# A two-layer hybrid encoder step on one core: the gate and up quadrants are loaded through GpSimd's queue

## The chip, the cores and the metric

The kernel runs on 1 of the 8 cores of one Trainium2 chip. The metric is the device time of one execution in microseconds (us). Engines are named as the profile names them: PE is TensorE's matmul side and PEld its weight load, DVE is VectorE, ACT is ScalarE, POOL is GpSimd, SP is SyncE. SP and POOL also have queues from which loads from HBM are issued.

## The reference

A step of a streaming encoder for 560 frames (512 new ones, 32 of a running stream, 16 meta frames) with a model width of 1024. Two layers, a GLA mixer and an MLA mixer, each stand between two half-step SwiGLU blocks; all is float32. The SwiGLU block is what the change touches:

```python
def swiglu_half(h, norm_w, w_gate, w_up, w_down):
    hn = rmsnorm(h, norm_w)
    return h + 0.5 * ((jax.nn.silu(hn @ w_gate) * (hn @ w_up)) @ w_down)
# per layer i: swiglu_half (ffn1), mixer (GLA for i = 0, MLA for i = 1), swiglu_half (ffn2); D_FF = 2816
```

## The kernel before, in words

Frames lie on the free dimension, features on the 128 partitions; the residual `h` stays on the core. A float32 product is made of three passes on float32r halves: every weight tile is cut into `whi` (ACT, line 331) and `wlo` (DVE, line 332, the rest after `whi`), both from pools of four buffers, and `mm` (line 370) multiplies whi by x-high (line 378), wlo by x-high (379) and whi by x-low (381).

**The four FFNs.** `ffn(1,0)`, `ffn(2,0)`, `ffn(1,1)` and `ffn(2,1)` run in this order, with the GLA mixer between the first two and the MLA mixer between the last two. Each has 11 steps of `gate_up` (line 467), two 128-column tiles of the hidden layer at a time. A step is a Strassen-like product: seven products of quadrants instead of eight. `quads` (line 435) brings the four quadrants r11, r12, r21, r22 of gate and up weights (each a tile `fr` of 128 x 1024 float32, 512 KB, loaded by `quadrant`, line 354, as two DMAs of 128 x 512, one for gate and one for up), adds them on DVE (line 451, four adds `fr<-fr` per step) and yields seven weight tiles in turn. The tiles `fr` come from a pool of six buffers, and each step takes five (the fifth holds a sum), so the load of a quadrant waits until DVE has finished with an earlier tile in that buffer.

**Down weights.** `down` (line 544) is cut into 16 pieces per group of steps; each loads its weights through `load` (line 334) into a tile `raw` (two buffers) and adds into `h` (line 556). The pieces of a group are woven between the products of the next group (`between`, line 579). The groups have 2, 4, 4, 4 and 8 tiles of the hidden layer; the first is one step long, and the pieces of the first group are short. The first two quadrants of a later FFN are also loaded ahead into `raw` tiles by `first_weights` (line 348).

**Queues.** All weight loads, quadrants and `raw` alike, are issued by SP, one after the other. An instruction on a queue that waits for its buffer holds up all that stand behind it there. POOL issues no load; it has some 110 small instructions in the two mixers (lines 616 to 645, 753 to 788, 913, 955, 1033, 1067, 1118 to 1123). ACT issues some constants and outputs. The scheduler of the language sets the final order on each engine, so that SP's quadrant loads and `raw` loads alternate within a step.

Of the kernel before, what the change touches and what calls it, by code (L numbers as in the profile page):

```python
# [289 lines left out]
class Net:  # L290
# [61 lines left out]
        return self.whole(raw)  # L352

    def quadrant(self, t, i, l, f, q):
        for j, x in enumerate("gu"):
            off, n = PLAN[x, i, l, f + q // 2]
            src = self.a["W"][off:off + P * n].rearrange("(p k c) -> p k c", p=P, k=2)[:, q % 2]
            self.nc.sync.dma_start(t[:, 512 * j:512 * j + 512], src)

    def whole(self, src):  # L360
        hi = self.w.tile([P, 8, P], F32R, name="whi", tag="whi")
# [1208 lines left out]
```

## Time and profile before

| what | value |
|---|---|
| median of 3 runs | 2117.19 us (2110.93 to 2117.34) |
| time of the profiled execution | 2109.41 us |
| its span, first to last instruction | 2107.5 us |
| outside the span | 1.9 us |
| PE busy, share of the span | 2026.0 us, 96% |
| DVE busy | 1643.2 us, 78% |
| ACT busy | 1018.4 us, 48% |
| POOL busy | 51.4 us, 2% |
| granted TensorE clock, mean | 0.982 |
| loads of 128 x 512 quadrant halves | 352 `fr<-W` and 12 `raw<-W`, 256 KB each |

The profile is of one execution, and all times within it are microseconds from the start of its span. A group row has the source line, the engine, the operation, the tiles out<-in, the shape and the count, then the busy time and the mean of one in ns, then the engine's idle time before them and what ended it. "SPq" is SP's queue. A line of the chain of waits has the start, the length and what was running. A row of the waits has the total in us, how many times, and the longest. The mixers lie at about 380 to 690 us and 1420 to 1720 us; the FFNs are the rest.

### The profile page before, as it was taken

How to read it: one execution, taken by the hardware profiler on the slowest of the kernel's cores; microseconds unless marked ns; L12 is line 12 of the kernel's file. 1: busy time of each engine (PE TensorE's matmuls, PEld its weight loads, DVE VectorE, ACT ScalarE, POOL GpSimd, SP SyncE). 2: the span in 40 equal slices, each digit the busy share in tenths (PEclk: the TensorE clock that was granted, in tenths of full speed). 3: DMA queues.
4: the chain of work that ended last, by engine and by line, in shares of the span. 5: the costliest groups of instructions: out<-in, count | busy, mean ns of one | idle time of the engine just before them, and what ended most of it. 6: DMA issues, size and time to landing. Idle time of an engine off the chain costs nothing.

```text
span 2107.5 us, 38039 instructions
## 1 busy us (share of the span) xinstructions
PE 2026.0 (96%) x15290; PEld 1980.2 (94%) x15290; DVE 1643.2 (78%) x3097; ACT 1018.4 (48%) x1822; POOL 51.4 (2%) x117
## 2 busy tenths in 40 slices
PE   5999999999999899999989999999999979999997
PEld 5999999989999799999979999999988969999997
DVE  8887878556658888788778877886788788878884
ACT  6444445455445444445545444454575454444451
POOL 0000000101110000000000000000210000000000
PEclk8999999999999899999989999999999989999998
DMA  3323222222221332322222322222211223232221
GB/s 131 106 87 107 93 96 78 77 68 71 73 80 55 108 103 82 106 86 91 81 95 96 105 92 91 95 83 92 61 51 59 71 86 100 90 111 91 96 72 62
DMA packets 93633, 183.29 MB, mean 87 GB/s; under 512 B 10433, under 2 KB 22081, under 8 KB 93457
## 3 DMA queue, kind: packets, MB, share of 16 engines
q1 hardware_dynamic: 89632, 176.24, 26.1%
q10 hardware_dynamic: 3824, 4.63, 0.7%
q8 instruction: 120, 1.97, 0.4%
q14 instruction: 57, 0.46, 0.1%
HBM read 176.84 MB, written 3.99 MB: 86 GB/s over the span
## 4 chain that ended last, share of the span: by engine, by line
PE 82%; DVE 10%; ACT 3%; DMA 2%; issue 2%; SPq 0%; POOL 0%; DVEq 0%; ACTq 0%; POOLq 0%
PE Y L381 8%; PE Y L378 8%; PE Y L379 8%; PE A L379 5%; PE A L381 5%; PE A L378 5%; PE ps L378 4%; PE ps L381 4%; PE ps L379 4%; PE B L378 3%; PE B L379 3%; PE B L381 3%; PE C L379 3%; PE C L381 3%; PE C L378 3%; DVE wlo L332 3%
## 5 line engine op out<-in xcount | busy, mean ns | idle before, releaser
L332 DVE TENSOR_TENSOR wlo<-fr,whi 128x1024 fp32r<-128x1024 f32 x302 | 363.9, 1216 | 17.2 <-ACT whi L331 17.0
L378 PE MATMUL Y<-ah,whi 128*128 128x280 f32 (+1 forms) x1408 | 373.8, 291 | 1.9 <-ACT ah L331 1.0
L379 PE MATMUL Y<-ah,wlo 128*128 128x280 f32 (+1 forms) x1408 | 373.4, 292 | 0.0
L331 ACT CAST whi<-fr 128x1024 fp32r<-128x1024 f32 x302 | 313.3, 1049 | 92.9 <-PE C L381 34.6
L378 PE MATMUL A<-x,whi 128*128 128x280 f32 (+1 forms) x1056 | 286.3, 296 | 29.5 <-ACT whi L331 29.5
L379 PE MATMUL A<-x,wlo 128*128 128x280 f32 (+1 forms) x1056 | 285.7, 296 | 1.0 <-DVE wlo L332 1.0
L378 PEld LDWEIGHTS Y<-ah,whi 128*128 128x128 f32 x1408 | 265.2, 188 | 3.4 <-ACT ah L331 1.7
L556 DVE SCALAR_TENSOR_TENSOR h<-Y,h 128x280 f32<-128x280 f32 (+1 forms) x320 | 140.9, 443 | 161.9 <-PE Y L381 161.2
L379 PEld LDWEIGHTS Y<-ah,wlo 128*128 128x128 f32 x1408 | 265.4, 188 | 0.0
L332 DVE TENSOR_TENSOR wlo<-raw,whi 128x512 fp32r<-128x512 f32 (+5 forms) x237 | 203.6, 861 | 76.7 <-ACT whi L331 71.9
L331 ACT CAST whi<-raw 128x512 fp32r<-128x512 f32 (+5 forms) x237 | 176.0, 744 | 173.4 <-PE ps L381 55.2
L381 PE MATMUL Y<-al,whi 128*128 128x280 f32 (+1 forms) x1408 | 233.9, 292 | 0.0
L378 PEld LDWEIGHTS A<-x,whi 128*128 128x128 f32 x1056 | 203.9, 193 | 31.1 <-ACT whi L331 31.1
L451 DVE TENSOR_TENSOR fr<-fr 128x1024 f32<-128x1024 f32 x176 | 214.5, 1219 | 20.4 <-DMA fr<-W 18.1
L379 PEld LDWEIGHTS A<-x,wlo 128*128 128x128 f32 x1056 | 203.7, 193 | 1.7 <-DVE wlo L332 1.4
L381 PEld LDWEIGHTS Y<-al,whi 128*128 128x128 f32 x1408 | 201.2, 189 | 0.0
L378 PE MATMUL B<-x,whi 128*128 128x280 f32 (+1 forms) x704 | 188.6, 293 | 3.4 <-ACT whi L331 3.4
L379 PE MATMUL C<-x,wlo 128*128 128x280 f32 (+1 forms) x704 | 187.1, 292 | 3.5 <-DVE wlo L332 3.5
L379 PE MATMUL B<-x,wlo 128*128 128x280 f32 (+1 forms) x704 | 187.4, 292 | 0.8 <-DVE wlo L332 0.8
L378 PE MATMUL C<-x,whi 128*128 128x280 f32 (+1 forms) x704 | 187.4, 291 | 0.6 <-ACT whi L331 0.6
L381 PE MATMUL A<-x,whi 128*128 128x280 f32 (+1 forms) x1056 | 181.2, 294 | 0.0
L490 ACT COPY r<-A 128x560 f32<-128x560 f32 (+1 forms) x132 | 82.2, 623 | 174.1 <-PE A L381 173.8
(368 smaller groups left out, 4059.2 us busy)
## 6 DMA issues: line engine op xcount, KB each, us to landing
fr<-W SPq DMA_DIRECT2D x352, 256.0 KB, 3.4
raw<-W SPq DMA_DIRECT2D x80, 512.0 KB, 3.5
raw<-W SPq DMA_DIRECT2D x112, 256.0 KB, 2.9
raw<-W SPq DMA_DIRECT2D x40, 128.0 KB, 2.1
h<-xT SPq DMA_DIRECT2D x3, 560.0 KB, 7.6
raw<-W SPq DMA_DIRECT2D x4, 384.0 KB, 3.1
o_y<-h SPq DMA_DIRECT2D x8, 136.0 KB, 2.2
o_y<-h ACTq DMA_DIRECT2D x8, 136.0 KB, 1.9
```

Of the source, the lines that this page charges most:

```text
L331: self.nc.scalar.copy(hi, src)
L332: self.nc.vector.tensor_tensor(lo, src, hi.bitcast(F32), op=ALU.subtract)
L378: f(hi[:, b0 + k, :], xh[:, c], start=not more and k == 0, stop=False)
L379: f(lo[:, b0 + k, :], xh[:, c], start=False, stop=False)
L381: f(hi[:, b0 + k, :], xl[:, c], start=False, stop=k == n - 1)
L451: add = lambda out, x, y: nc.vector.tensor_tensor(out, x, y, op=ALU.add)
L490: nc.scalar.copy(r[:, :, :n], of[:, :, :n])
L556: nc.vector.scalar_tensor_tensor(self.h[:, m, c], Y[:, :n], 0.5, self.h[:, m, c], op0=ALU.mult, op1=ALU.add)
```

## The change

`quadrant` chooses a queue. Only the four quadrants of the very first step (`ffn(1,0)`, f = 0) stay on SP; all other quadrant halves, those of `first_weights` among them, are issued by POOL. Down weights, mixer weights and the inputs stay on SP. Sizes, tiles, buffers and arithmetic are as before. The lines below 355 move down by two, so 358 becomes 360.

```diff
     def quadrant(self, t, i, l, f, q):
+
+        queue = self.nc.sync if (i, l, f) == (1, 0, 0) else self.nc.gpsimd
         for j, x in enumerate("gu"):
             off, n = PLAN[x, i, l, f + q // 2]
             src = self.a["W"][off:off + P * n].rearrange("(p k c) -> p k c", p=P, k=2)[:, q % 2]
-            self.nc.sync.dma_start(t[:, 512 * j:512 * j + 512], src)
+            queue.dma_start(t[:, 512 * j:512 * j + 512], src)
```

SP's queue around the start of `ffn(2,0)`, before (W is the packed weight array; `fr` is a quadrant, `raw` a down or mixer weight, or a quadrant where line 358 stands):

```order
L341 DMA raw<-W 128x1024 x28
L358 DMA raw<-W 128x512 x4
L341 DMA raw<-W 128x1024 x2
L341 DMA raw<-W 128x256 x2
L358 DMA fr<-W 128x512 x18
L341 DMA raw<-W 128x256
L358 DMA fr<-W 128x512
L341 DMA raw<-W 128x256
L358 DMA fr<-W 128x512 x2
L341 DMA raw<-W 128x256
L358 DMA fr<-W 128x512 x2
L341 DMA raw<-W 128x256
```

The same queue at the same place now:

```order
L341 DMA raw<-W 128x816 x2
L341 DMA raw<-W 128x544
L341 DMA raw<-W 128x1024 x30
L341 DMA raw<-W 128x256 x8
L341 DMA raw<-W 128x512 x24
L341 DMA raw<-W 128x1024 x8
```

The quadrants are gone from it, and the `raw` loads stand one behind the other in the same order.

POOL's queue at the head of the program, before (the first rows of work are the constants of the GLA mixer, some 360 us into the run):

```order
L1561 MEMSET const-uint8-127 128x1
L1566 UNCONDITIONAL_BRANCH [waits barrier_Pool_Activation_PE_DVE_SP_gather]
L616 MEMSET aT_4687 128x128 [waits DVE_49,PE_49,Activation_49]
L616 MEMSET aT_4688 128x128
L616 MEMSET aT_4689 128x128
```

And now:

```order
L1563 MEMSET const-uint8-127 128x1
L1568 UNCONDITIONAL_BRANCH [waits barrier_Pool_Activation_PE_DVE_SP_gather]
L360 DMA fr<-W 128x512 x2
L360 DMA fr<-W 128x512 [waits DVE_49]
L360 DMA fr<-W 128x512
L360 DMA fr<-W 128x512 [waits DMAHW3_49,DMAHW4_49,DVE_49,Activation_49]
L360 DMA fr<-W 128x512
```

The first quadrant of the second step (f = 2) has no wait before it, and stands at the head of POOL's queue from the start of the run; on SP it stood behind the inputs and the whole first step.

POOL's queue at the turn from the MLA mixer to `ffn(2,1)`, before: the last copies of the mixer, and then nothing to the end.

```order
L1123 CAST qrs<-x 64x32 [waits DVE_49,Pool_49]
L1118 CAST ptl<-x 128x32 [waits DVE_49,Pool_49]
L1118 CAST pth<-x 128x32 [waits Activation_49]
L1118 CAST ptl<-x 128x32 [waits DVE_49]
L1566 UNCONDITIONAL_BRANCH
```

And now (the names behind "waits" are semaphores of engines and of earlier loads, DMASW those of POOL's own):

```order
L360 DMA raw<-W 128x512
L360 DMA fr<-W 128x512 [waits DMASW4_49,DVE_49,PE_49]
L360 DMA fr<-W 128x512 [waits DMASW5_49]
L360 DMA fr<-W 128x512 x2
L360 DMA fr<-W 128x512 [waits DMASW0_49]
L360 DMA fr<-W 128x512 [waits DMASW1_49]
L360 DMA fr<-W 128x512 [waits DMASW2_49]
L360 DMA fr<-W 128x512 [waits DMASW3_49]
L360 DMA fr<-W 128x512 [waits DMASW4_49,Pool_49]
L360 DMA fr<-W 128x512 [waits DMASW5_49]
L360 DMA fr<-W 128x512 [waits DMASW6_49,DVE_49]
```

The eight halves of the first step's four quadrants stand on POOL one after the other behind a single wait for room, as they stood on SP. The sequences of PE, DVE and ACT are the same as before but for a few neighbours that change places in some steps.

## Prediction

> **What bounds the kernel now.** First the page's head: which engine is full. Then the busy time in each FFN (the four windows are `ffn(1,0)`, `ffn(2,0)`, `ffn(1,1)`, `ffn(2,1)` without their ends; columns: length, busy time and count of PE, PEld, DVE, ACT, POOL, then clock, DMA share, GB/s).
>
> ```profile
> span 2107.5 us, 38039 instructions
> PE 2026.0 (96%) x15290; PEld 1980.2 (94%) x15290; DVE 1643.2 (78%) x3097; ACT 1018.4 (48%) x1822; POOL 51.4 (2%) x117
> 50.00:435.00 385.00, 381.28 (x2918) 377.82 (x2919) 299.77 (x463) 180.57 (x300) 9.45 (x27) 0.99 0.28 91
> 745.00:1080.00 335.00, 332.20 (x2569) 331.65 (x2567) 269.67 (x414) 156.33 (x241) 0.00 (x0) 1.00 0.29 93
> 1080.00:1420.00 340.00, 332.35 (x2545) 331.14 (x2546) 279.83 (x410) 159.68 (x248) 0.18 (x1) 0.98 0.29 93
> 1715.00:2080.00 365.00, 351.74 (x2774) 350.24 (x2774) 291.06 (x439) 167.08 (x261) 0.00 (x0) 0.98 0.30 95
> ```
>
> PE is busy for 97 to 99% of these stretches, at 0.98 to 1.00 of its clock, while loads keep the DMA engines busy for 0.28 to 0.30. DVE is the second: 80 to 82%. So the question is not how long SP's queue waits, but whether PE ever waits for a quadrant. Next the waits: PE's largest, SP's two largest, and DVE's for quadrants.
>
> ```profile
> PE A L378 <- ACT whi L331: 29.5, 6, 8.8
> SPq L341 <- DVE wlo L332: 826.0, 159, 30.4
> SPq L358 <- DVE wlo L332: 517.2, 109, 24.0
> DVE fr L451 <- DMA fr<-W: 18.1, 16, 2.5
> ```
>
> SP waits 1343 us at the two load lines, but for DVE to free a buffer, and another queue has to wait for the same buffers. DVE waits 18.1 us for quadrants in 16 places. PE's 29.5 us are six waits, and by their places they lie at the start of an FFN:
>
> ```profile
> PE A L378 <- ACT whi L331: 15.3, 2, 8.8
> PE A L378 <- ACT whi L331: 3.8, 1, 3.8
> PE A L378 <- ACT whi L331: 6.2, 1, 6.2
> ```
>
> 15.3 us lie in the first 25 us of the run, 3.8 us each at the start of `ffn(2,0)` and `ffn(1,1)`, 6.2 us at that of `ffn(2,1)`. In the middle of an FFN PE does not wait for loads. The change can hardly win time there; what it can lose is the margin of the few loads that come in just in time.
>
> **What a load costs on POOL.** The change moves 356 of 364 loads of 128 x 512 (352 `fr` and 12 `raw`, less the 8 of the first step) from SP to POOL. SP issues one in about 0.43 us:
>
> ```profile
> fr<-W SPq DMA_DIRECT2D x352, 256.0 KB, 3.4
> L358 SPq DMA_DIRECT2D fr<-W x10: 327/430/500, 1713.7 to 1717.8; - x10
> DMA to landing us min/median/max: 2.9/5.9/6.8
> ```
>
> The ten loads at the start of `ffn(2,1)` take 327 to 500 ns each to issue; the quickest is down 2.9 us after the start of its issue, so 2.6 us after its end. The trace has no load on POOL. The nearest rows are POOL's own instructions on 128 x 512:
>
> ```profile
> 443.44 1.04 POOL L788 TENSOR_TENSOR qS<-qg,fac 128x512 f32<-128x512 f32 x1
> 448.27 1.24 POOL L788 TENSOR_TENSOR kS<-kd,fac 128x512 f32<-128x512 f32 x1 [3.79 <-DVE kd L781]
> ```
>
> I bound one issue on POOL by 0.43 us below (no dearer than on SP) and 1.24 us above, and take 1.04 us, the nearer of POOL's own rows, what it takes over a tile of this size undisturbed; SP's row is another engine's. In an FFN 88 loads come in 335 us or more, one in 3.8 us, so POOL is no bottleneck by rate.
>
> [...]
>
> **Part by part.** (1) *Start of the run.* POOL's first two loads wait for nothing, so 512 KB for the second step enter the DMA engines beside the inputs and the first quadrants.
>
> ```profile
> 2.66 5.00 DMA fr<-W
> 7.74 1.04 ACT whi L331
> 3.00:15.00 12.00, 5.51 (x27) 5.20 (x28) 7.50 (x14) 9.58 (x19) 0.00 (x0) 1.00 1.02 339
> ```
>
> The chain starts with a quadrant half that lands at 7.66 us and its cast at 7.74; from 3 to 15 us the DMA engines are full (share 1.02, 339 GB/s). 524,288 bytes at 339 GB/s are 1.55 us, which the first quadrant and the inputs come later if POOL's loads share the engines with them. Between 0 and 1.55 us; I take +1.5, since the chain is DMA and its users up to PE's start.
>
> (2) *The tight place of each FFN.* In the third and fourth step the short down pieces fill little PE time and DVE has no rest. There one quadrant's buffer comes free late. The chain in `ffn(1,1)`, then DVE and PE as they go on:
>
> ```profile
> 1149.31 1.24 DVE wlo L332
> 1150.57 0.33 SPq L358
> 1150.94 3.88 DMA fr<-W
> 1154.89 1.24 DVE fr L451
> 1158.96 1.22 DVE L332 TENSOR_TENSOR wlo<-fr,whi 128x1024 fp32r<-128x1024 f32 x1
> 1160.23 0.40 PE L379 MATMUL B<-x,wlo 128*128 128x280 f32 x1 [0.17 <-DVE wlo L332]
> ```
>
> DVE frees the buffer at 1150.55, SP issues both halves, the second lands at 1154.82 (4.27 us after the release), DVE adds at 1154.89, cuts the next tile at 1158.96, and PE waits 0.17 us for just that tile. So a later landing is paid in full. The same DMA stands ahead of DVE's add in two other FFNs (the first is taken to be alike, from the code):
>
> ```profile
> 759.30 3.93 DMA fr<-W
> 1792.09 1.24 DVE fr L451
> ```
>
> On POOL: 1150.55 + 2 issues + the time from issue to landing, which is 2.6 us at best and 3.88 - 0.43 = 3.45 us here. With 1.04 and the middle, 3.0, that is 1155.6, 0.8 us later; with 0.43 and 2.6 it is 0.8 us earlier, which PE, not idle there, can't use: 0; with 1.24 and 3.45 it is 1.7 later. Four places: +3.2, from 0 to 6.8.
>
> (3) *Start of `ffn(2,1)`.* Eight halves must be down before DVE's four adds.
>
> ```profile
> 1716.90 0.43 SPq L358
> DMA to landing us min/median/max: 6.2/6.3/6.4
> 1723.48 5.00 DVE L451 TENSOR_TENSOR fr<-fr 128x1024 f32<-128x1024 f32 x4
> ```
>
> The first is issued at 1713.68, the eighth at 1716.90, which lands 6.4 us later at 1723.3, and DVE starts at 1723.48. POOL: 1713.68 + 8 x 1.04 + 2.6 = 1724.6, so +1.1 against 1723.48; at 0.43 per issue it stays with the transfers, 0; at 1.24 and 3.45 it is 1727.05, +3.6. PE's 6.2 us wait there grows by as much. At the starts of `ffn(2,0)` and `ffn(1,1)` there is room:
>
> ```profile
> L358 SPq DMA_DIRECT2D fr<-W x10: 328/430/432, 679.1 to 683.3; - x10
> 693.37 4.99 DVE L451 TENSOR_TENSOR fr<-fr 128x1024 f32<-128x1024 f32 x4
> ```
>
> 679.1 + 8 x 1.04 + 2.6 = 690.0, before DVE's add at 693.37: 0. `ffn(1,1)` has more room, its adds come over 20 us after the first issue.
>
> (4) *What leaves SP's queue.* The `raw` loads no longer stand behind quadrants, nor quadrants behind them. PE has no wait in mid-FFN to give back: 0. POOL's small work in the mixers stands behind loads long issued: 0. The two instructions that choose the queue are Python: 0.
>
> Sum: 1.5 + 3.2 + 1.1 = +5.8 us, from 0 to 1.55 + 6.8 + 3.6 = +12. The profiled execution took 2109.41 us, so it would take 2115.2; the median of the runs shown is 7.8 us above it, 2117.19, and the forecast against it is **2123 us**. About 0.3%, or 6.4 us, is what a measurement of this kernel can tell from no change, so the forecast lies just within.
>
> **The rivals.** *A: issuing on POOL holds up DVE.* The trace has both sides of it:
>
> ```profile
> 361.41 0.73 DVE L501 TENSOR_TENSOR gu<-gu,yn 128x560 f32<-128x560 f32 x1
> 361.39 0.49 POOL L616 MEMSET aT<- 128x128 f32 x3 [360.94 <-PE B L381]
> 448.52 2.06 DVE L332 TENSOR_TENSOR wlo<-raw,whi 128x1024 fp32r<-128x1024 f32 x1
> 359.91 1.23 DVE L332 TENSOR_TENSOR wlo<-raw,whi 128x1024 fp32r<-128x1024 f32 x1
> ```
>
> Beside POOL's memsets, which only write, a two-input DVE instruction keeps its 0.73 us. Beside POOL's kS at 448.27, which reads, the cut takes 2.06 instead of 1.23. If each load costs DVE 0.83 us, an FFN's 88 cost 73 us, and DVE's idle time in `ffn(1,1)`, 340 - 279.83 = 60, is used up: 13 us over; and the tight steps, some three with 24 loads, have no idle time to use: 24 x 0.83 = 20. Four FFNs make 52 to 80 us; I take 50 beside the other terms, 2173. It decides once a load takes more from DVE than its idle share, 60/88 = 0.7 us. Against it: an issue need not read a tile.
>
> [...]
>
> *B: POOL's issues are held up behind DVE, or long in themselves.* If each waits for one DVE cut, it takes 1.04 + 1.22 = 2.26 us. Start of `ffn(2,1)`: 1713.68 + 18.1 + 2.6 = 1734.4, +10.9; `ffn(2,0)`: 679.1 + 20.7 = 699.8, +6.4; the tight places 4.5 + 2.6 - 4.27 = +2.8 each, 11.3; the start 1.5. Together +30: 2147. It turns the forecast into a loss from 1.1 us per issue on. For it: DVE is busy 80%. Against it: the most that the trace shows of this is kS, 0.20 us longer than qS while DVE's cut ran beside it.
>
> [...]
>
> *C: SP's freed queue brings quadrants earlier where PE does wait.* All of 3.8 + 3.8 + 6.2 = 13.8 us gone gives 2103. Against it: the loads at 1713.68 start when room comes free, and at the two others DVE's adds come last.
>
> **How the numbers follow.** The forecast's case has 0.68: 0.46 within 0.3%, 0.20 slower by more (its upper terms), 0.02 faster. A has 0.12 and B 0.14, both slower; C 0.06, faster. That is faster 0.08, same 0.46, slower 0.46. The forecast's own range is 2117 to 2129; as slower cases hold so much, the range goes from 2111 to 2150, which takes in B and leaves out A and C, 0.18.
>
> **What would show it.** In the profile after: POOL's issue rows near 1.0 us (A and B aside); the cut `wlo<-fr,whi` unchanged at 1216 ns mean (A: 1300 or more); PE waiting about 1 us for DVE near 1160 and 7.3 instead of 6.2 at `ffn(2,1)`; the first cast near 9.2 instead of 7.74. The forecast is wrong if POOL's loads take above 1.3 us each, or if PE's waits for `whi` fall.

## The result, and the profile after

The changed kernel takes 2122.86 us (median of 15 runs, 2118.57 to 2125.53), the kernel before 2117.19 us (15 runs, 2109.8 to 2119.69). The ratio is 1.0029, 95% interval 1.0019 to 1.0039: slower by 4 to 8 us, 0.3%. The profiled execution took 2121.41 us.

The page of the changed kernel: its head, then the two costliest groups of DVE and POOL (busy us, mean ns of one, then the idle time ahead of them and who ended most of it), then a row of DMA issues (count, size, median us from issue to landing). Lines of the file stand 2 lower than before, from 358 on (358 is 360, 378 is 380).

```profile
span 2119.5 us, 38101 instructions
PE 2032.5 (96%) x15290; PEld 1983.4 (94%) x15290; DVE 1642.3 (77%) x3097; ACT 1018.5 (48%) x1822; POOL 241.0 (11%) x473
L332 DVE TENSOR_TENSOR wlo<-fr,whi 128x1024 fp32r<-128x1024 f32 x302 | 364.2, 1218 | 16.4 <-ACT whi L331 16.4
L360 POOL DMA_DIRECT2D fr<-W x344 | 183.0, 537 | 1187.0 <-DVE wlo L332 840.6
fr<-W POOLq DMA_DIRECT2D x344, 256.0 KB, 3.8
```

An issue occupies POOL for 0.537 us, half of what the forecast took; a load is down 3.8 us after the start of its issue, against 3.4 on SP. DVE's cut takes 1218 ns, as before (1216), so the issues on POOL cost DVE's cut nothing that shows. That settles rival A. What an issue itself reads or writes on the core no run here shows. Rival B falls with 0.537 us and a longest issue of 0.677 us. The waits of the changed kernel (total us, times, longest) show whom the loads reach:

```profile
DVE fr L453 <- DMA fr<-W: 32.9, 24, 2.6
PE A L380 <- ACT whi L331: 30.6, 6, 9.7
```

DVE waits 32.9 us for quadrants instead of 18.1; PE's waits for `whi` did not fall (29.5 before), so nothing was won (rival C). The longest, the first matmul's, grew from 8.8 to 9.7.

**A place that was forecast.** The tight place of `ffn(2,0)`, before and then after (start, length, engine, instruction, and in brackets the idle time ahead and who ended it):

```profile
763.35 2.48 DVE L451 TENSOR_TENSOR fr<-fr 128x1024 f32<-128x1024 f32 x2 [1.97 <-DMA fr<-W]
768.68 0.40 PE L379 MATMUL B<-x,wlo 128*128 128x280 f32 x1 [0.25 <-DVE wlo L332]
```

```profile
766.00 1.60 POOL L360 DMA_DIRECT2D fr<-W  x3 [2.49 <-issue]
771.22 2.49 DVE L453 TENSOR_TENSOR fr<-fr 128x1024 f32<-128x1024 f32 x2 [2.50 <-DMA fr<-W]
776.55 0.39 PE L381 MATMUL B<-x,wlo 128*128 128x280 f32 x1 [0.79 <-DVE wlo L332]
```

DVE waits 0.53 us longer for the quadrant, and PE 0.54 us longer for DVE: the delay is paid in full. But not all of it is the load's. The chain that ends in DVE's add, after (start, length, what was running):

```profile
767.07 3.67 DMA fr<-W
770.83 0.40 issue
```

Before, the second half had landed at 763.23 and DVE began 0.12 us later; now it lands at 770.75 and DVE begins 0.47 us later, 0.40 of it without a wait that the profile shows. So 0.35 us of the delay at this place lie behind the landing. They come back in c2 and p2, the other profiles of this order on DVE in which the place is as late, and their cause stays open.

**A place that was not forecast.** Some 64 us before the end of `ffn(2,1)` two halves of a quadrant are loaded one after the other. Before, then after:

```profile
1983.21 0.80 SPq L358 DMA_DIRECT2D fr<-W  x2
1987.03 2.48 DVE L451 TENSOR_TENSOR fr<-fr 128x1024 f32<-128x1024 f32 x2 [0.21 <-DVE h L556]
```

```profile
1995.13 1.07 POOL L360 DMA_DIRECT2D fr<-W  x2 [6.83 <-DVE wlo L332]
2000.69 2.49 DVE L453 TENSOR_TENSOR fr<-fr 128x1024 f32<-128x1024 f32 x2 [2.22 <-DMA fr<-W]
```

DVE now waits 2.22 us there, and the steps around it take 1.7 us longer. POOL starts 0.28 us after DVE frees the buffer (the median of 106 loads that a cut released; on SP 0.02, of 89) and needs 0.27 us more for two issues; that is 0.5 us, and not 2. The cause of the rest is looked for below. Two of the four FFNs without their ends, after:

```profile
71.00:368.00 297.00, 296.31 (x2297) 1.00 0.30 94
736.00:1034.00 298.00, 295.58 (x2287) 1.00 0.29 92
```

These are windows of PE alone (length, PE's busy time, clock, DMA share, GB/s). The granted clock is full in them (1.00), as it is in the other two and in all four before, and the times from step to step can be compared between kernels to some hundredths of a microsecond (the middle steps agree to 0.02 us in all kernels but e1, g and e2, below); most of the table below rests on that.

### The profile page after: what moved, and what is told of

It is laid out like the page before. It is cut to its first block, busy times and chain, and to the rows that moved or that the text cites. A ratio compares the mean times of both kernels' runs of the same rounds, so it can differ in the third digit from the quotient of the medians.

```text
span 2119.5 us, 38101 instructions
## 1 busy us (share of the span) xinstructions
PE 2032.5 (96%) x15290; PEld 1983.4 (94%) x15290; DVE 1642.3 (77%) x3097; ACT 1018.5 (48%) x1822; POOL 241.0 (11%) x473
## 4 chain that ended last, share of the span: by engine, by line
PE 79%; DVE 11%; ACT 3%; DMA 3%; issue 2%; POOL 1%; SPq 0%; DVEq 0%; ACTq 0%; POOLq 0%
PE Y L383 8%; PE Y L380 8%; PE Y L381 8%; PE A L381 5%; PE A L383 5%; PE A L380 5%; PE ps L380 4%; PE ps L383 4%; PE ps L381 4%; DVE wlo L332 4%; PE B L380 3%; PE B L381 3%; PE C L381 3%; PE B L383 3%; PE C L383 3%; PE C L380 3%
## 5 line engine op out<-in xcount | busy, mean ns | idle before, releaser
L332 DVE TENSOR_TENSOR wlo<-fr,whi 128x1024 fp32r<-128x1024 f32 x302 | 364.2, 1218 | 16.4 <-ACT whi L331 16.4
L331 ACT CAST whi<-fr 128x1024 fp32r<-128x1024 f32 x302 | 313.2, 1049 | 90.7 <-PE C L383 28.1
L360 POOL DMA_DIRECT2D fr<-W x344 | 183.0, 537 | 1187.0 <-DVE wlo L332 840.6
L453 DVE TENSOR_TENSOR fr<-fr 128x1024 f32<-128x1024 f32 x176 | 214.8, 1220 | 34.1 <-DMA fr<-W 32.9
```

Source lines behind the costliest of these rows:

```text
L331: self.nc.scalar.copy(hi, src)
L332: self.nc.vector.tensor_tensor(lo, src, hi.bitcast(F32), op=ALU.subtract)
L360: queue.dma_start(t[:, 512 * j:512 * j + 512], src)
L453: add = lambda out, x, y: nc.vector.tensor_tensor(out, x, y, op=ALU.add)
```

## The theories

- **T1**, the prediction's: what costs is POOL's later landing, at places without margin alone.
- **T2**: what costs is the order. With POOL in the loads, the scheduler moved two additions of DVE and a copy of ACT in each of three FFNs and one matmul in `ffn(2,1)`, and SP's queue holds down weights alone.
- **T3**: the clock. Between 390 and 735 us, in the first mixer, the changed kernel lost 5.3 us where no quadrant is waited for, and its granted clock was 0.96 there instead of 0.98.
- **T4**, formed on the way, after e6: a load is late when a fetch of PE's own instructions falls into its transfer.

T4 came from one row of the page, alike before and after, of DMA queues (packets, MB, share of 16 engines):

```profile
q8 instruction: 120, 1.97, 0.4%
```

120 packets of 16 KB, of about 1 us each. They come once per 127 matmuls (111 to 152 in the profile before); on DVE and ACT the counts between two packets scatter far more (14 to 72 and 9 to 50), so they are taken to be PE's instructions. With 15290 matmuls and as many weight loads in the profile before, a packet comes to 127 of each. T4 supposes that a load has landed when its last packet is through, and that a packet behind a fetch has to wait. In the place above, the packets of the changed kernel between 1998.3 and 1999.4 us are these, and behind them those of SP and POOL from 1999.3 to 2000.6:

```profile
q1 hardware_dynamic: 8, 0.03, 33.6%
q8 instruction: 1, 0.02, 5.5%
q0 software_dynamic: 7, 0.01, 4.5%
```

```profile
q1 hardware_dynamic: 74, 0.30, 66.5%
q0 software_dynamic: 3, 0.01, 3.9%
```

The fetch runs from 1998.35 to 1999.33. At 1998.3 all but nine of the 160 packets of POOL's pair had begun; the last three begin at 1999.32, 1999.74 and 2000.10, and the second half has landed at 2000.57 only. The packets of q1 are those of SP's next down-weight load, which begin at 1999.11 and run beside these three. So the fetch holds the last packets up by about 0.7 us, and what follows, with SP's load beside them, is not parted from it here. Before, the fetch came at 1986.3, when 4 packets of SP's were left:

```profile
q8 instruction: 1, 0.02, 6.2%
q1 hardware_dynamic: 4, 0.00, 1.1%
```

Over both profiles of before, pairs of halves with no other load in flight need 3.70 us from the first issue to the second landing (median of 46, 3.29 to 4.08), and 4.71 us (10, 4.36 to 5.30) where a fetch starts 1.0 to 2.9 us after the first issue. POOL's, over both profiles of after: 3.91 (22, 3.60 to 4.27) and 4.55 (6, 4.32 to 5.25). The bounds of 1.0 and 2.9 were chosen with the pairs in view, and a fetch outside them can count or not: with one 3.3 us after the first issue, one of SP's pairs took 5.78 us and another 4.03.

## The experiments

One table holds what all profiles say. DVE runs 416 instructions that add into `h` in every kernel; between two of them, of the same numbers in all, lies the same work. The table gives how much longer such a stretch took than in the quickest of all these kernels, in us: the tight places of the FFNs (numbers 2 to 18, 114 to 130, 194 to 210, 322 to 336), and the ends (61 to 65, 172 to 178, 252 to 257, and for `ffn(2,1)` 368 to 381 with the place shown above, and 381 to 385). "First" is the time at which PE's first matmul on the first quadrant starts, "start" PE's wait at the start of `ffn(2,1)`. The middle steps between these are the same to 0.02 us in all kernels but e1 (0.25 in `ffn(1,0)`, 2.27 in `ffn(2,1)`), g (0.13 and 0.43 there) and e2 (0.10 in `ffn(1,0)`).

| kernel | first | tight (1,0), (2,0), (1,1), (2,1) | start | end (1,0), (2,0), (1,1) | end (2,1) | ratio, interval |
|---|---|---|---|---|---|---|
| before | 8.84 | 0.00, 0.56, 0.49, 0.30 | 6.2 | 0.19, 0.15, 0.17 | 0.00, 0.57 | 1 |
| c1_before_again | 8.92 | 0.00, 0.09, 0.25, 0.21 | 6.8 | 0.33, 0.19, 0.11 | 0.00, 0.65 | one run |
| after | 9.74 | 0.71, 1.10, 0.55, 0.50 | 6.4 | 0.21, 1.53, 0.55 | 1.71, 0.90 | 1.0029 (1.0019 to 1.0039) |
| c2_after_again | 9.72 | 0.55, 1.26, 0.71, 1.06 | 7.6 | 0.23, 1.27, 0.38 | 1.82, 1.20 | 1.0030 (1.0016 to 1.0044) |
| e1_pool_quarters | 9.97 | 1.17, 1.26, 0.97, 1.02 | 12.2 | 0.73, 7.85, 0.00 | 1.71, 0.00 | 1.0102 (1.0081 to 1.0122) |
| e2_pool_one_dma | 11.21 | 0.73, 0.61, 0.67, 0.99 | 6.0 | 1.45, 1.77, 2.70 | 0.49, 0.60 | 1.0046 (1.0028 to 1.0063) |
| e4_start_only | 9.63 | 0.00, 0.46, 0.41, 0.15 | 6.4 | 1.14, 0.03, 0.08 | 0.00, 0.96 | one run |
| e5_last_step_only | 8.72 | 0.49, 0.07, 0.56, 0.19 | 7.0 | 0.16, 1.58, 0.32 | 0.00, 1.14 | 1.0008 (0.9993 to 1.0023) |
| e6_all_but_last | 8.68 | 0.35, 0.57, 0.56, 1.07 | 7.0 | 0.29, 1.98, 0.12 | 1.88, 0.57 | 1.0013 (1.0002 to 1.0024) |
| p1_before_shift16 | 8.78 | 0.00, 0.12, 0.44, 0.33 | 6.6 | 0.01, 0.00, 0.27 | 0.64, 0.56 | 1.0008 (0.9994 to 1.0023) |
| p2_after_shift46 | 9.66 | 0.65, 1.31, 0.77, 1.59 | 7.6 | 0.06, 0.85, 0.11 | 0.20, 0.70 | 1.0025 (1.0012 to 1.0037) |
| p3_before_shift73 | 8.81 | 0.35, 1.17, 0.77, 0.46 | 6.4 | 0.00, 0.03, 0.08 | 0.00, 1.75 | 1.0014 (1.0003 to 1.0025) |
| g_steps246_sp | 8.86 | 0.10, 0.00, 0.00, 0.31 | 7.5 | 0.07, 1.95, 0.52 | 1.67, 0.98 | 1.0027 (1.0017 to 1.0038) |
| m1_middle_only | 8.40 | 0.02, 0.06, 0.16, 0.00 | 6.0 | 0.50, 0.04, 0.11 | 0.00, 0.68 | 0.9999 (0.9988 to 1.0010) |

### c1_before_again and c2_after_again: both kernels once more

No edit.

> The kernel before, unchanged, profiled once more. Between the 100th microsecond or so and the end of the first GLA mixer (stretch 390 to 724 us of the first profile) the changed kernel lost 5.3 us to the kernel before, and there are no loads of quadrants there that PE waits for. T1 (POOL's later landing at places without margin) and T2 (the changed order) both call this stretch chance: how long the granted clock is halved differs from execution to execution. Then this second profile of before differs from its first by some us in the mixers and at the very end (1 to 6 us), and by under 0.1 us inside the FFNs. T3 (the change lengthens the half-clock stretches): this profile agrees with the first, half-clock time 79 us in all, within 2 us.

> The changed kernel, unchanged, profiled once more and timed. T1 and T2: the losses inside the FFNs come back at the same places and within 0.1 us (start of the run +1.3, last steps of ffn(2,0) +1.3, of ffn(2,1) +2.0, tight places 0.2 to 0.7 each), while the 5.3 us of the first GLA mixer change by some us either way. T3: the 5.3 us come back too. Ratio to before about 1.003.

PE from 390 to 735 us in four profiles (first before, then after, then before again, then after again; clock, DMA share and GB/s at the end):

```profile
390.00:735.00 345.00, 330.12 (x2403) 0.98 0.24 77
```

```profile
390.00:735.00 345.00, 329.43 (x2362) 0.96 0.23 74
```

```profile
390.00:735.00 345.00, 330.16 (x2379) 0.97 0.23 75
```

```profile
390.00:735.00 345.00, 329.97 (x2400) 0.98 0.23 77
```

Counted from step to step on DVE, the kernel before itself lost 3.2 us there the second time, and the changed kernel lost 0.4 instead of 5.3. Over the whole execution the clock was granted at half for 79.0 and 90.7 us in the two profiles of before, and for 90.3 and 76.9 us in those of after. So that loss was chance between executions, and T3 falls. The losses inside the FFNs came back at the same places (table), within 0.3 us rather than the 0.1 expected, 0.56 at the tight place of `ffn(2,1)`. The kernel before itself moved by 0.47 us at that of `ffn(2,0)`. A difference of half a microsecond at one place of one profile is therefore within chance.

### e1_pool_quarters and e2_pool_one_dma: more issues, or fewer

```diff
-            queue.dma_start(t[:, 512 * j:512 * j + 512], src)
+            w = 512 if queue is self.nc.sync else 256
+            for c in range(0, 512, w):
+                queue.dma_start(t[:, 512 * j + c:512 * j + c + w], src[:, c:c + w])
```

> As the changed kernel, but each 128x512 half that POOL loads is split into two loads of 128x256, so that a quadrant is four issues instead of two: the bytes, the tiles and who waits for whom stay. T1: if an issue costs POOL 0.54 us whatever its size, a quadrant is complete about 1.1 us later at each place without margin; the end of each FFN, the tight places and the start of ffn(2,1) lose about 1 us more each, in all some 8 to 12 us above the changed kernel, ratio to before 1.006 to 1.009. If an issue costs by its bytes, nothing changes: 1.003. T2 (it is the order and the separate queues, not when POOL's loads land): 1.003, as the changed kernel. T3: the half-clock time decides, 1.003 with the FFN losses unchanged.

```diff
-        for j, x in enumerate("gu"):
-            off, n = PLAN[x, i, l, f + q // 2]
-            src = self.a["W"][off:off + P * n].rearrange("(p k c) -> p k c", p=P, k=2)[:, q % 2]
-            queue.dma_start(t[:, 512 * j:512 * j + 512], src)
+        off, n = PLAN["g", i, l, f + q // 2]
+        src = self.a["W"][off:off + 2 * P * n].rearrange("(j p k c) -> p j k c", j=2, p=P, k=2)[:, :, q % 2]
+        queue.dma_start(t.rearrange("p (j c) -> p j c", j=2), src)
```

> As the changed kernel, but both halves of a quadrant in one load of 128x2x512 (512 KB) on POOL: one issue instead of two, the same bytes. T1: if an issue costs 0.54 us whatever its size, the quadrant is complete about 0.5 us earlier, half or so of the FFN losses goes, ratio to before 1.001 to 1.002; if an issue costs by its rows (256 instead of 128), it takes about 1.07 us, the first half starts no earlier, and the ratio stays at 1.003 or rises. T2: 1.003. T3: 1.003, with the half-clock time deciding.

The group and the row of issues of e1, with its start of `ffn(2,1)`; then those of e2:

```profile
L362 POOL DMA_DIRECT2D fr<-W x688 | 365.6, 538 | 1025.2 <-DVE wlo L332 718.6
fr<-W POOLq DMA_DIRECT2D x688, 128.0 KB, 2.9
1731.73 10.06 POOL L362 DMA_DIRECT2D fr<-W  x19 [2.48 <-issue]
1743.06 2.48 DVE L455 TENSOR_TENSOR fr<-fr 128x1024 f32<-128x1024 f32 x2 [6.06 <-DMA fr<-W]
```

```profile
L359 POOL DMA_DIRECT2D fr<-W x172 | 124.6, 725 | 1244.0 <-DVE wlo L332 903.6
fr<-W POOLq DMA_DIRECT2D x172, 512.0 KB, 4.4
```

Half the bytes cost the same 538 ns, twice the rows 725 ns. Doubling the issues made the kernel slower by 1.0%, more than the 0.6 to 0.9 expected: POOL needs 10 us for 19 issues at the start of `ffn(2,1)`, where PE's wait doubles to 12.2, and the end of `ffn(2,0)` loses 7.85, where about 1 us more was expected; why it is so much was not followed up. That is what T1 forecasts in kind, but e1 does not part it from T2: the scheduler moved some 40 instructions of DVE and 25 of ACT against the changed kernel, some of them at that end, so its order is not the one for which T2 forecast 1.003. The merged load was expected to win back half of the loss; instead it is slower still (1.0046), with the order of the changed kernel on DVE, ACT and PE. Its one issue is shorter than two, but with no other load and no fetch beside it it is down after 4.12 us (median of 12), where a pair was down after 3.91; and with the first quadrants, which SP loads, merged too, the first matmul waits 11.2 us. That step of T1 was wrong.

### e4_start_only, e5_last_step_only, e6_all_but_last: parts of the change

```diff
-        queue = self.nc.sync if (i, l, f) == (1, 0, 0) else self.nc.gpsimd
+        queue = self.nc.gpsimd if (i, l, f, q) == (1, 0, 2, 0) else self.nc.sync
```

> The kernel before, but the two halves of the first quadrant of the second step of ffn(1,0) are loaded by POOL at the start; all other loads stay on SP. T1: these 512 KB enter the DMA engines beside the inputs and the first quadrants, so PE's first matmul waits about 9.7 us instead of 8.8 to 8.9, as in the changed kernel, and nothing changes in the four FFNs: PE's waits there and the times between their steps stay within 0.1 us of the kernel before, the half-clock stretches aside. T2 (the order of the queues): if the start's loss comes from the loads of the inputs that SP issues in another order, the first matmul stays at 8.8 to 8.9 us.

```diff
+        queue = self.nc.gpsimd if f == FT - 2 else self.nc.sync
```

> The kernel before, but the quadrants of the last step of each FFN alone (32 of 356 loads) go to POOL. T1: the losses at the ends of the FFNs come back and nothing else: about 1.1 to 1.4 us at the end of ffn(2,0), 0.2 to 0.4 at that of ffn(1,1), 2.0 to 2.5 at that of ffn(2,1), none at the start of the run or at the tight places, in all 3.5 to 4.3 us, ratio to before 1.0015 to 1.002. T2 (what costs is that the loads of down weights on SP stand in another order than the quadrants, in the whole FFN): a last step alone changes little, under 1 us, ratio 1.0005 at most.

```diff
+        queue = self.nc.sync if (i, l, f) == (1, 0, 0) or (i, l, f, q) == (1, 0, 2, 0) or f == FT - 2 else self.nc.gpsimd
```

> The complement: as the changed kernel, but the last step of each FFN and the first quadrant of the second step of ffn(1,0) are loaded by SP again; the other 318 or so loads stay on POOL. T1: what is left is the tight places (0.2 to 0.7 each, about 1.5 us in all) and the start of ffn(2,1) (0.2 to 1.2): 1.7 to 2.7 us, ratio to before 1.0008 to 1.0013; PE's first matmul at 8.8 to 8.9 us, and the ends of the FFNs within 0.2 us of the kernel before. T2: nearly all loads are still in the changed order, so nearly all of the loss stays, 5 us or more, ratio 1.0025 to 1.003.

PE's waits for `whi` in the first 26 us of e4, then of e6 (total, times, longest):

```profile
PE A L380 <- ACT whi L331: 16.1, 2, 9.6
```

```profile
PE A L380 <- ACT whi L331: 15.1, 2, 8.7
```

The start is as expected: two early loads of POOL cost the first matmul 0.7 to 0.9 us, and without them it is gone. The ends are not. With the last step alone on POOL, `ffn(2,0)` loses 1.58 but `ffn(2,1)` only 0.5; with the last step back on SP both lose as much as ever (1.98; 1.88 and 0.57). e5 also loses 0.49 at the tight place of `ffn(1,0)`, where none was expected: the loads there stand on SP and meet no fetch, but the late pair took 3.74 us instead of 3.22. And e4, without a load of POOL near, loses 0.9 us at the end of `ffn(1,0)`, where e5 and e6 don't. So the loss at the ends does not simply follow the step whose loads POOL issues: single loads are late. Of the last four down-weight loads of each FFN in the nine profiles up to here, the ten into which a fetch started 0 to 2.6 us after their issue took 3.7 to 5.1 us, those without a fetch near 3.44 (median of 108). Hence T4. e6's ratio, 1.0013, lies in the range expected, but the ends that it was to spare were not spared: in its one profile the places of the table add up to 5.6 us more than before, where the interval of the ratio ends at 5.1.

At the end of `ffn(2,0)` it is the down weights on SP that meet a fetch; ACT's cast before, and after:

```profile
1017.96 1.05 ACT L331 CAST whi<-raw 128x1024 fp32r<-128x1024 f32 x1 [0.70 <-DMA raw<-W]
```

```profile
1027.18 1.05 ACT L331 CAST whi<-raw 128x1024 fp32r<-128x1024 f32 x1 [2.05 <-DMA raw<-W]
```

ACT waits 1.35 us longer. Of these, 0.74 are the transfer: 4.30 us with a fetch 0.73 us after its issue, instead of 3.56 with one at 3.15. The other 0.61 are its start. DVE waits that much longer for the last quadrants of the FFN, which POOL loads (before, then after), and frees the buffer of the down weights later:

```profile
988.68 1.23 DVE L451 TENSOR_TENSOR fr<-fr 128x1024 f32<-128x1024 f32 x1 [2.01 <-DMA fr<-W]
```

```profile
997.17 1.23 DVE L453 TENSOR_TENSOR fr<-fr 128x1024 f32<-128x1024 f32 x1 [2.63 <-DMA fr<-W]
```

In e6 this load starts no later than before, and its whole loss is a transfer of 5.36 us. The fetch, too, comes 1.8 us earlier against the work around it in both profiles of after than in those of before, though PE's order is the same up to there; no run shows why.

### p1, p2, p3: the fetches moved, the loads left where they are

The kernel before (p1, p3) or the changed one (p2) with 16, 73 or 46 added matmuls of one column at the very start, while PE waits; `one` is the tile of ones. All other instructions keep their order. p1:

```diff
     net.psum(True)
+    one = net.ones.bitcast(mybir.dt.bfloat16)
+    for n in (15, 1):
+        out = net.bank("Y")
+        for _ in range(n):
+            net.nc.tensor.matmul(out[:32, :1], one[:, :32], one[:, :1], start=True, stop=True)
```

> The kernel before, all loads on SP, with 16 added matmuls of one column whose result nobody uses, while PE waits for the first quadrant. They move each fetch of PE's instructions (16 KB on one DMA engine, one per 127 matmuls or so) about 2 us earlier against the rest of the program; the order on all engines stays. T4 (a load is late when such a fetch falls into its transfer): the first of the last four down-weight loads of ffn(2,0), which took 3.6 us with the fetch 3.1 us after its issue, now meets it and takes 4.2 to 5.1, and PE waits 1 to 1.7 us there (0.3 before); at the end of ffn(1,1) 0.2 to 0.4 more; nothing else, 1 to 2 us in all, ratio 1.0005 to 1.001. T1 alone (only POOL's later landing matters): nothing changes at any place, ratio 1.000.

> The changed kernel, with 46 such matmuls: fetches about 6 us earlier. T4: the two loads near the ends of ffn(2,0) and ffn(2,1) that met a fetch no longer do: the down-weight load at ffn(2,0) takes 3.4 to 3.7 instead of 4.2 to 4.3 us, PE's wait there falls from 1.4 to 1.6 to 0.2 to 0.6; the second half of the quadrant about 64 us before the end of ffn(2,1) takes 3.3 to 3.5 instead of 4.9 to 5.0, and 1.3 to 1.8 us of the loss there goes; some 0.5 us may come at the last step of ffn(2,1), where a fetch now falls in. In all 2 to 3 us less than the changed kernel, ratio to before 1.0015 to 1.002. T1 alone: the losses at both places stay, ratio 1.003.

> The kernel before, all loads on SP, with 73 such matmuls: fetches about 9.5 us earlier, so that one falls into the late quadrant of the tight place in ffn(2,0) (759 us of the first profile) and one in ffn(1,1) (1151 us). T4: those quadrants land 0.6 to 1.5 us later, and PE waits about as much longer at each, 1.2 to 3 us in all, ratio 1.0005 to 1.0015; all without a load on POOL. T1 alone: nothing changes, ratio 1.000.

p1 missed its target: the fetch came 0.86 us ahead of the load at the end of `ffn(2,0)`, 4.0 us earlier than before and not 2, and nothing was lost there. It met another, unplanned, the pair of the place shown above, now with all loads on SP; DVE's wait in p1:

```profile
1989.60 2.49 DVE L451 TENSOR_TENSOR fr<-fr 128x1024 f32<-128x1024 f32 x2 [1.15 <-issue]
```

It was 0.21, and the stretch took 0.64 us longer. The ratio of p1, 1.0008 (0.9994 to 1.0023), takes in what both theories expected. p2 does the opposite. The same pair on POOL; and all packets from 1997.9 to 2001.9 us by queue, now without a fetch among them:

```profile
1997.96 1.07 POOL L360 DMA_DIRECT2D fr<-W  x2 [6.83 <-DVE wlo L332]
2002.01 2.48 DVE L453 TENSOR_TENSOR fr<-fr 128x1024 f32<-128x1024 f32 x2 [0.71 <-DMA fr<-W]
```

```profile
q0 software_dynamic: 160, 0.52, 40.8%
```

DVE's wait falls from 2.22 to 0.71, the loss from 1.7 or 1.8 to 0.20, with the load on POOL as before; SP's next down-weight load was issued 3.02 us after the pair in both kernels, so it is the fetch that makes the difference; with none, POOL's packets are through before SP's begin. At the end of `ffn(2,0)` the loss falls from 1.4 to 0.85: the load of down weights takes 3.53 us again, and the 0.66 us that ACT still waits longer than before are its later start. In `ffn(1,1)` the loss falls to 0.11. A new one appears at the tight place of `ffn(2,1)` (1.59). The ratio, 1.0025, lies above the 1.0015 to 1.002 expected, and its interval takes in both these and 1.003; the places decide, not the ratio. p3, all loads on SP, with fetches put into two tight places; the one in `ffn(2,0)`:

```profile
772.26 2.49 DVE L451 TENSOR_TENSOR fr<-fr 128x1024 f32<-128x1024 f32 x2 [2.57 <-DMA fr<-W]
777.59 0.39 PE L379 MATMUL B<-x,wlo 128*128 128x280 f32 x1 [0.86 <-DVE wlo L332]
```

PE waits 0.86 us there, more than in the changed kernel (0.79), without a load on POOL. Before and c1 lost 0.56 and 0.09 in that stretch, p3 1.17; at `ffn(1,1)` it lost 0.77 against 0.49 and 0.25, and 1.75 at the last step of `ffn(2,1)`, where a down-weight load that met a fetch took 5.0 us. The ratio is 1.0014, as expected. T4 stands.

### g_steps246_sp: the order of before, most loads on POOL

```diff
+        queue = self.nc.sync if (i, l, f) == (1, 0, 0) or f in (2, 4, 6) else self.nc.gpsimd
```

> The changed kernel with the quadrants of the steps f = 2, 4 and 6 of every FFN on SP again. With that, the order on DVE, ACT and PE is that of the kernel before, row for row, while some 258 loads, those of the ends of the FFNs among them, stay on POOL. T1 with T4 (late landing, and fetches): the loss at the end of ffn(2,0) (1.1 to 1.4) and at that of ffn(2,1) (2.0 to 2.5) stays, start and tight places are as before, in all 3.5 to 4.5 us, ratio 1.0015 to 1.002. T2 (the changed order costs it): ffn(2,1) loses 0.6 us at most, as where only the last step was on POOL, ratio 1.0008 at most.

1.0027, above the expected 1.0015 to 1.002. The tight places are as quick as ever, the ends lose 1.95, 0.52 and 1.67 with the order of before. T2 is refuted for the ends as far as the order on DVE, ACT and PE goes; that SP's queue holds down weights alone is the same there as in the changed kernel. At the tight places the order changes only together with the queue, so their shares there were not parted.

### m1_middle_only: loads with margin

```diff
+        queue = self.nc.gpsimd if 8 <= f <= 14 else self.nc.sync
```

> The kernel before, with the quadrants of the steps f = 8 to 14 of each FFN alone (128 loads) on POOL, where they land some 0.5 us before DVE or ACT want them or PE has work in hand; start, tight places and last steps stay on SP, and the order on DVE, ACT and PE is that of before. T1 with T4: no place without margin is touched, so the four FFNs lose at most 0.5 us in all against the kernel before, PE's first matmul at 8.8 to 8.9 us, ratio 1.000, at most 1.0005. If each load on POOL had a price of its own (the changed kernel's 0.3% spread over its 356), 128 would cost 0.0011, 2.2 us, and it would show in these middle steps.

```profile
fr<-W POOLq DMA_DIRECT2D x128, 256.0 KB, 3.7
766.12 2.49 DVE L453 TENSOR_TENSOR fr<-fr 128x1024 f32<-128x1024 f32 x2 [1.46 <-DMA fr<-W]
```

The second line is the tight place of `ffn(2,0)`, whose loads stand on SP here. The ratio is 0.9999 (0.9988 to 1.0010): 128 loads on POOL cost nothing that can be measured where nobody waits for them. The interval just leaves out the 1.0011 of a price per load, and none of the places between the tight ones and the ends lost more than 0.02 us. No version beat the kernel before by more than the measurement can tell.

## Why the prediction was right, and where not

The time (2123.0 against 2122.86) and the direction were right; the sum behind it was right in part. Terms as the prediction put them, against after and c2 less before and c1 (means of two profiles each, from the table):

1. *Start of the run*, +1.5: measured +0.85. The mechanism held (e4 has it, e6 has not); all 512 KB ahead of it would have been 1.5, so not all of these bytes came ahead; how many did was not measured. The first cast started at 8.64 and 8.62 us, where the prediction looked for about 9.2.
2. *Tight places*, +3.2: measured +2.3 (0.63, 0.86, 0.26, 0.52). The issue on POOL is 0.54 us, not 1.04; but POOL starts 0.28 us after the release, which was not in the sum, and a pair lands later after its first issue. For a pair without a fetch that makes 0.28 + 3.91 against 0.02 + 3.70, 0.5 us. The 0.86 of `ffn(2,0)` holds 0.35 more, which lie behind the landing. PE's wait near 1160, of which the prediction asked about 1 us, became 0.23 and 0.38.
3. *Start of `ffn(2,1)`*, +1.1: measured +0.5, with 1.2 us between two profiles of one kernel, so this term is not told from nothing. The eight issues of 0.54 us did not delay the eighth half: it was down 9.43 us after the first issue began (1725.25 to 1734.68), against 9.61 before (1713.68 to 1723.30); e1 shows what twice as many cost.
4. *SP's freed queue*, 0: held.

The step that failed is that the sum gives an FFN no place without margin but its start and its tight place, and nothing at its end. The ends have others, and they cost +3.7 us: 1.2 in `ffn(2,0)`, 0.3 in `ffn(1,1)`, 1.8 and 0.4 in `ffn(2,1)`, none in `ffn(1,0)`. Two things add up there. POOL's later landing is passed on, to DVE and by it to the down weights (about 0.55 of the 1.2 us at the end of `ffn(2,0)`, means of two profiles each). And a load falls into a fetch of PE's instructions, which adds the other 0.66 there and some 1.5 us in `ffn(2,1)`, where POOL's half a microsecond brings it into the fetch. The 0.4 of the last step of `ffn(2,1)` was not parted; p3, with all loads on SP, lost more there. So that the time came out right is luck: terms 1 to 3 were 2.2 us too large, a term of 3.7 us was missing, and the two errors partly cancel. The sum of all is 7.4 us by these profiles, within the interval of the ratio (4.0 to 8.3), where the medians differ by 5.7.

The quickest load on POOL was down 2.9 us after the start of its issue and the median load after 3.8, so 2.4 and 3.3 us after its end, where the forecast took 2.6 to 3.45. From the start of an issue to its first packet the traces have 1.24 us on POOL (median of 101 loads of after, issued with no other load in flight) and 0.96 on SP (196, before), which is 0.28 us less.

## What to carry to other kernels

The queue change was priced here by the few loads that somebody waits for: 128 loads with margin cost nothing that could be measured, and some ten places without it cost 0.3%. A pair of loads from POOL lands some 0.5 us later than one from SP here: POOL reacts 0.28 us later, and each issue over 128 rows takes 0.54 us, with rows of 1 KB as with rows of 2 KB. Splitting the loads in two made the kernel slower (1.0102 against 1.0029). Merging two didn't pay either (1.0046), as the merged load is down after 4.12 us and a pair after 3.91. And a margin under 1 us was luck here: one tight place moved by 0.56 us between two profiles of one kernel, and at the end of `ffn(2,1)` a shift of half a microsecond brought in another delay of some 1.5 us. So read a margin from more than one profile.

## What the runs showed of the hardware that was not expected

- What is taken to be PE's instructions comes in packets of 16 KB (120 in the profile before), one in about 127 matmuls, of about 1 us each. A pair of loads with such a packet 1.0 to 2.9 us behind its first issue landed later by the medians: 1.0 us on SP (4.71 against 3.70), 0.6 on POOL (4.55 against 3.91). Sixteen to 73 matmuls of no use at the start moved delays of 0.6 to 1.5 us from one place of the program to another.
- An issue on POOL took 537 ns in the mean for 128 rows of 2 KB (after), 538 ns for 128 rows of 1 KB (e1), and 725 ns for 256 rows of 2 KB (e2).
- The time from 390 to 735 us, in the first mixer, differs between executions of one kernel by up to 5 us, with a granted clock of 0.96 in one and 0.98 in the other, while the middle steps of the FFNs agree to 0.02 us.
- Why the fetch at the end of `ffn(2,0)` moved by 4 us in p1, where 2 were expected of 16 matmuls, stays open; so does why a load at the end of `ffn(2,0)` took 5.36 us in e6, where the fetch began 3.3 us after its issue, late in the transfer: one at 3.15 us (before) or 3.21 (c1) left that load at 3.6.
